# A one-core hybrid attention, pooling and expert layer: first norm by halves of tokens, activation table and token loads rearranged, five subtractions moved from VectorE to GpSimd

## The chip, the core and the metric

The kernel runs on one core of a Trainium2 chip. The metric is the device time of one execution in microseconds (us). An execution of the kernel before takes 1541.66 us (median of three). Five engines run side by side, each through its own queue in order: TensorE (PE in the profile, PEld its weight loads), VectorE (DVE), ScalarE (ACT), GpSimd (POOL) and SyncE (SP), which here issues nearly all transfers from memory.

## The reference

One layer for 512 tokens of 1024 channels. The opening of the kernel, where most of the change lies, computes the first norm, its modulation, and the first columns of one wide projection.

```python
def rms_norm(x, g):
    x32 = x.astype(jnp.float32)
    y = x32 * lax.rsqrt(jnp.mean(x32 * x32, axis=-1, keepdims=True) + EPS)
    return (y * g.astype(jnp.float32)).astype(x.dtype)
...
        ada = c @ w_ada[layer] + b_ada[layer]
        shift1, scale1, gate1, shift2, scale2, gate2 = [a[:, None, :] for a in jnp.split(ada, 6, axis=-1)]

        h = rms_norm(x, g_norm1[layer]) * (1.0 + scale1) + shift1
        z = h @ w_in[layer]
        zq, zk, zv, ziq, zik, ziw, zp, zg = jnp.split(z, cuts, axis=-1)
        q = rms_norm(zq.reshape(B, S, N_HEADS, HEAD_DIM), g_q[layer])
        k = rms_norm(zk, g_k[layer])
...
        mixed = (g_attn * y_attn + g_pool * y_pool) @ w_out[layer]
        x = x + gate1 * mixed

        h2 = rms_norm(x, g_norm2[layer]) * (1.0 + scale2) + shift2
        x = x + gate2 * peer_ffn(h2, w_peer_q[layer], peer_subkeys[layer], peer_u[layer], peer_v[layer])
```

In between stand sparse attention over 128 chosen keys, a pooling mixer with four windows, and, after the second norm, an expert lookup of 128 experts a token, which takes most of the time.

## The kernel before

Channels lie on the 128 partitions and tokens along the row: `x` is eight slices `xs[:, d, :]` of 128 channels by 512 tokens. A product in full precision is made of three passes of reduced-precision matmuls: each operand is split into a high part (ACT copies it into the shorter format, `split` L138, `modulate` L157) and a low part, which is the operand less its high part (DVE, L139, L158). `passes` (L171 to L173) multiplies high by high, high weights by low activations, and low weights by high activations.

The opening, with the names that the profile shows:

- SP loads `col`, `crow` and the eight slices of x (L249), then in turn two rows of `w_ada` (`wada`, L105) and one block of `w_in` (`ws`, L165), five times, then the remaining `wada`. Four buffers hold `wada`, three hold `ws`: the next transfer of a kind is issued when an earlier buffer has been used up.
- ACT squares each slice (`n1sq`, L144), DVE adds the squares up (`n1p`, L146), and PE sums over channels by a product with `ones` (`n1s`, L150 and L151; the eighth square goes to PE directly). A load of ACT's function table (L256) stands in ACT's queue ahead of the eighth square.
- `rsqrt` (L126) takes the root of the sum for all 512 tokens: three ACT functions (L129 to L131) and one refining step on DVE (L132 to L134) whose second instruction, L133, is a `tensor_scalar`.
- For each slice d DVE forms two columns of `ada` (L106, an instruction of 128x1024 that also sums, followed by a short read of its accumulator), adds the bias (L267), forms the gain `a1` (L268), the normed slice `n1f` (L156) and, after ACT has made the high part `hh` (L157), the low part `hl` (L158). While d is below five, DVE also forms the low part `wls` of the weight block that has come (L139).
- PE multiplies each finished slice with every block that has come: five blocks by eight slices by three passes, 120 matmuls of 128x512, in an order that a scheduler set when the kernel was built.

The scheduler places instructions on each engine by its own estimate of times, so the code does not tell the order; the rows of the next section but one do. Later parts call the same helpers: `rsqrt` for keys, queries and the second norm, `split` for all weight blocks, `square` and `modulate` for the second norm (L508 to L525).

## Time and profile before

| | |
|---|---|
| three executions | 1541.14, 1541.66, 1542.42 us |
| the profiled execution | 1543.48 us, of which the span from first to last instruction is 1541.7 us |
| mean granted clock of TensorE | 0.993 of full speed |
| busy | PE 97%, PEld 84%, DVE 84%, ACT 42%, POOL 21% of the span |

The page of a profile tells busy shares over the whole span. A stage is read with the table of busy time by stretches (a row has the stretch, its length, then PE, PEld, DVE, ACT and POOL), the timeline of one engine (start, duration, engine, line, operation, output and inputs, shapes, count, and in brackets how long the engine sat idle before and what ended that), and the chain of waits. On one engine the start of the next instruction less the start of this one is what an instruction costs; its duration is a little longer, since neighbours overlap at the ends.

### The profile page before, as it was taken

The page shows a single profiled execution, that of the slowest core. Times are in us where ns is not written, and L with a number is a line of the kernel's source. Part 1 is how long each engine was busy: PE and PEld are TensorE (multiplying, and loading weights), DVE is VectorE, ACT ScalarE, POOL GpSimd, SP SyncE. Part 2 cuts the span into 40 slices and gives each one's busy share as a digit, 9 for nine tenths or more (in the row PEclk, how much of TensorE's full clock was granted, in tenths as well). Part 3 has the DMA queues.
Part 4 walks back from the last instruction along what each step waited for, and adds up shares of the span by engine and source line. Part 5 has one row for each costly group of instructions (what it writes and reads, how often), then busy time and mean ns, then how long its engine had stood idle before and what let it go on. Part 6 is the DMA issues. An engine that isn't in the chain of part 4 may idle for free.

```text
span 1541.7 us, 22240 instructions
## 1 busy us (share of the span) xinstructions
PE 1497.2 (97%) x7889; PEld 1301.8 (84%) x7889; DVE 1294.3 (84%) x2672; ACT 647.2 (42%) x991; POOL 324.8 (21%) x318
## 2 busy tenths in 40 slices
PE   5999999999999999999999999999999999999998
PEld 3778787877789999899888999999999999998886
DVE  7799886767999999993778888888888888888887
ACT  4653555533444454453333333333333333333332
POOL 0000000000000000001123444444444444453320
PEclk8999999999999999999999999999999999999999
DMA  8412673523236666689889999999999999998884
GB/s 313 178 55 89 233 237 92 197 97 110 70 110 209 201 182 206 213 249 331 316 317 351 332 344 357 317 360 320 354 346 336 358 316 362 331 348 315 317 302 147
DMA packets 158545, 393.91 MB, mean 256 GB/s; under 512 B 13537, under 2 KB 68449, under 8 KB 158306
## 3 DMA queue, kind: packets, MB, share of 16 engines
q1 hardware_dynamic: 121570, 258.26, 48.1%
q0 software_dynamic: 36864, 134.23, 24.8%
q8 instruction: 62, 1.02, 0.3%
q14 instruction: 49, 0.40, 0.1%
HBM read 358.75 MB, written 33.69 MB: 255 GB/s over the span
## 4 chain that ended last, share of the span: by engine, by line
PE 79%; DVE 14%; DMA 3%; ACT 3%; issue 1%; SPq 0%; ACTq 0%; DVEq 0%
PE acc L807 31%; PE pse L556 6%; PE pse L555 6%; PE pse L554 6%; PE pse L570 4%; PE pse L572 4%; PE pse L571 3%; PE gm L667 3%; DMA v<-v 2%; DVE ule L534 2%; DVE bias L352 1%; PE po L471 1%; DVE m L351 1%; PE psga L173 1%; PE pso L171 1%
## 5 line engine op out<-in xcount | busy, mean ns | idle before, releaser
L732 POOL DMA_INDIRECT ur<-u,ei x128 | 156.6, 1224 | 605.5 <-DMA ad<-gelu 366.5
L807 PE MATMUL acc<-vl,Wh 128*128 128x512 f32 x768 | 237.1, 389 | 0.5 <-DVE vl L799 0.4
L807 PE MATMUL acc<-vh,Wl 128*128 128x512 f32 x768 | 237.3, 390 | 0.0
L807 PE MATMUL acc<-vh,Wh 128*128 128x512 f32 x768 | 236.6, 389 | 0.0
L740 POOL DMA_INDIRECT vr<-v,ei x128 | 165.2, 1290 | 213.7 <-DVE sacc L745 185.0
L799 DVE TENSOR_TENSOR vl<-v,vh 128x1024 fp32r<-128x1024 f32 x128 | 156.8, 1225 | 62.6 <-ACT vh L797 62.4
L556 PE MATMUL pse<-h2h,ule 128*128 128x384 f32 x552 | 185.2, 335 | 0.7 <-DVE ule L534 0.7
L554 PE MATMUL pse<-h2h,uhe 128*128 128x384 f32 x552 | 184.5, 334 | 1.2 <-ACT uhe L533 1.2
L555 PE MATMUL pse<-h2l,uhe 128*128 128x384 f32 x552 | 184.6, 334 | 0.0
L796 ACT ACTIVATE Wh<-gelu 128x384 fp32r<-128x384 f32 x106 | 55.6, 525 | 287.9 <-PE acc L807 170.2
L807 PEld LDWEIGHTS acc<-vl,Wh 128*128 128x128 f32 x768 | 143.9, 188 | 31.2 <-DVE vl L799 1.5
L807 PEld LDWEIGHTS acc<-vh,Wl 128*128 128x128 f32 x768 | 144.2, 188 | 30.0
L570 PE MATMUL pse<-h2h,uhe 128*128 128x384 f32 x472 | 168.2, 356 | 0.6 <-ACT gelu L579 0.6
L534 DVE TENSOR_TENSOR ule<-ue,uhe 128x1024 fp32r<-128x1024 f32 x128 | 156.0, 1218 | 15.2 <-ACT uhe L533 15.1
L572 PE MATMUL pse<-h2h,ule 128*128 128x384 f32 x472 | 161.6, 343 | 5.3 <-DVE ule L534 5.3
L745 DVE SCALAR_TENSOR_TENSOR sacc<-vr,wt,sacc 128x1024 f32<-128x1024 f32 x127 | 162.8, 1282 | 2.4
L807 PEld LDWEIGHTS acc<-vh,Wh 128*128 128x128 f32 x768 | 143.2, 188 | 24.5
L571 PE MATMUL pse<-h2l,uhe 128*128 128x384 f32 x472 | 159.2, 337 | 0.0
L533 ACT ACTIVATE uhe<-ue 128x1024 fp32r<-128x1024 f32 x128 | 134.5, 1051 | 58.4 <-PE pse L571 38.2
L734 DVE SCALAR_TENSOR_TENSOR ur<-ur,hx 128x1024 f32<-128x1024 f32 x128 | 150.8, 1220 | 0.9 <-DMA ur<-u,ei 0.9
L797 ACT ACTIVATE vh<-v 128x1024 fp32r<-128x1024 f32 x128 | 135.9, 1062 | 14.2 <-DMA v<-v 13.9
L554 PEld LDWEIGHTS pse<-h2h,uhe 128*128 128x128 f32 x552 | 103.6, 188 | 4.3 <-ACT uhe L533 1.7
(422 smaller groups left out, 2672.5 us busy)
## 6 DMA issues: line engine op xcount, KB each, us to landing
ue<-uT SPq DMA_DIRECT2D x128, 512.0 KB, 5.3
v<-v SPq DMA_DIRECT2D x128, 512.0 KB, 5.8
wada<-w_ada SPq DMA_DIRECT2D x48, 512.0 KB, 4.6
gd<-st SPq DMA_DIRECT2D x24, 1024.0 KB, 5.7
g<-gd SPq DMA_DIRECT2D x48, 512.0 KB, 8.0
ad<-gelu SPq DMA_DIRECT2D x22, 192.0 KB, 2.8
wgp<-w_in SPq DMA_DIRECT2D x8, 512.0 KB, 3.6
wga<-w_in SPq DMA_DIRECT2D x8, 512.0 KB, 4.4
```

The lines of the kernel that those rows point to most:

```text
L534: V.tensor_tensor(lo, src, hi.bitcast(F32), op=ALU.subtract)
L554: T.matmul(p, hi[:, k, :], h2h[:, k, :n], start=(k == 0), stop=False)
L555: T.matmul(p, hi[:, k, :], h2l[:, k, :n], start=False, stop=False)
L556: T.matmul(p, lo[:, k, :], h2h[:, k, :n], start=False, stop=(k == DT - 1))
L570: T.matmul(ps, hi[:, k, :], h2h[:, k, :ND], start=(k == 0), stop=False)
L571: T.matmul(ps, hi[:, k, :], h2l[:, k, :ND], start=False, stop=False)
L572: T.matmul(ps, lo[:, k, :], h2h[:, k, :ND], start=False, stop=(k == DT - 1))
L732: G.indirect_dma_start(out=ur, out_offset=None, in_=u, in_offset=bass.IndirectOffsetOnAxis(ap=ei3[:, k:k + 1], axis=0))
L740: G.indirect_dma_start(out=vr, out_offset=None, in_=v, in_offset=bass.IndirectOffsetOnAxis(ap=ei3[:, k:k + 1], axis=0))
L745: V.scalar_tensor_tensor(sacc, vr, wt[:, k:k + 1], sacc, op0=ALU.mult, op1=ALU.add)
L799: V.tensor_tensor(vl, vr, vh.bitcast(F32), op=ALU.subtract)
L807: T.matmul(acc[tb][i], x[:, t], y[:, i * 512:(i + 1) * 512], start=(c == 0 and n == 0), stop=(c == NEXP - 1 and n == 2))
```

## The change

Five things. The root of the first norm, its first modulated slice, and the last square are computed in two halves of 256 tokens (`CUT1 = 2`; `CUT2 = 1` leaves the second norm whole). The function table of the first norm is asked for at the start of ACT's queue instead of ahead of the eighth square, so that one load stands where two stood. x comes in four transfers of two slices each, from an array that the host lays out for it, in the opening and again ahead of the second norm. `rsqrt` loses its `tensor_scalar`: the factor it applied is multiplied into the gains in `col` once, at the start, by two small instructions (and into the factor that scales the queries' roots). And `load` takes an engine for the low part: for the first five blocks of `w_in` it is GpSimd.

```diff
--- before.py
+++ after.py
 SCALED = 14
+CUT1 = 2
+CUT2 = 1
...
+        V.tensor_scalar(col[:, C_G1:C_GQ], col[:, C_G1:C_GQ], -0.5 / D, None, op0=ALU.mult)
+        V.tensor_scalar(col[:, C_GK:C_GIK + 1], col[:, C_GK:C_GIK + 1], -0.5 / 64, None, op0=ALU.mult)
...
+        def pieces(n, cut):
+            return [slice(i * n // cut, (i + 1) * n // cut) for i in range(cut)]
+
+        def rsqrt(ps, scale, name, tag="rs", n=S, cut=1):
 
             r = tmp.tile([P, n], F32, tag=f"{tag}_r", name=f"{name}r", bufs=1)
             t = tmp.tile([P, n], F32, tag=f"{tag}_t", name=f"{name}t", bufs=1)
-            A.activation(t, ps, AF.Ln, bias=eps, scale=scale)
-            A.activation(r, t, AF.Exp, scale=-0.5)
-            A.activation(t, r, AF.Square)
-            V.scalar_tensor_tensor(t, ps, EPS / scale, t, op0=ALU.add, op1=ALU.mult)
-            V.tensor_scalar(t, t, -0.5 * scale, 1.5, op0=ALU.mult, op1=ALU.add)
-            V.tensor_tensor(r, r, t, op=ALU.mult)
+            for c in pieces(n, cut):
+                A.activation(t[:, c], ps[:, c], AF.Ln, bias=eps, scale=scale)
+                A.activation(r[:, c], t[:, c], AF.Exp, scale=-0.5)
+                A.activation(t[:, c], r[:, c], AF.Square)
+                V.scalar_tensor_tensor(t[:, c], ps[:, c], EPS / scale, t[:, c], op0=ALU.add, op1=ALU.mult)
+                V.scalar_tensor_tensor(r[:, c], t[:, c], -3.0 / scale, r[:, c], op0=ALU.add, op1=ALU.mult)
             return r
 
-        def split(hi, lo, src):
+        def split(hi, lo, src, engine=V):
             A.activation(hi, src, AF.Copy)
-            V.tensor_tensor(lo, src, hi.bitcast(F32), op=ALU.subtract)
+            engine.tensor_tensor(lo, src, hi.bitcast(F32), op=ALU.subtract)
 
         def square(part, src, d, name):
 
             sq = tmp.tile([P, S], F32, tag="sq", name=f"{name}{d}") if d else part
             A.activation(sq, src, AF.Square)
-            if 0 < d < DT - 1:
+            if d:
                 V.tensor_tensor(part, part, sq, op=ALU.add)
-            return sq
-
-        def square_sum(ps, part, last):
-            T.matmul(ps, ones, part, start=True, stop=False)
-            T.matmul(ps, ones, last, start=False, stop=True)
-
-        def modulate(src, rs, ga, shift, hi, lo, name):
+
+        def square_sum(ps, part, src, name, cut=1):
+
+            sq = tmp.tile([P, S], F32, tag="sq", name=name)
+            for c in pieces(S, cut):
+                A.activation(sq[:, c], src[:, c], AF.Square)
+                T.matmul(ps[:, c], ones, part[:, c], start=True, stop=False)
+                T.matmul(ps[:, c], ones, sq[:, c], start=False, stop=True)
+
+        def modulate(src, rs, ga, shift, hi, lo, name, cut=1):
 
             f = tmp.tile([P, S], F32, tag="nf", name=name)
-            V.scalar_tensor_tensor(f, src, ga, rs, op0=ALU.mult, op1=ALU.mult)
-            A.activation(hi, f, AF.Identity, bias=shift)
-            V.scalar_tensor_tensor(lo, f, shift, hi.bitcast(F32), op0=ALU.add, op1=ALU.subtract)
-
-        def load(src, kt, name, pool=wp):
+            for c in pieces(S, cut):
+                V.scalar_tensor_tensor(f[:, c], src[:, c], ga, rs[:, c], op0=ALU.mult, op1=ALU.mult)
+                A.activation(hi[:, c], f[:, c], AF.Identity, bias=shift)
+                V.scalar_tensor_tensor(lo[:, c], f[:, c], shift, hi[:, c].bitcast(F32), op0=ALU.add, op1=ALU.subtract)
+
+        def load(src, kt, name, pool=wp, engine=V):
 
             w = wp.tile([P, DT, P], F32, tag="w", name=f"w{name}")[:, :kt, :]
             hi = pool.tile([P, DT, P], F32R, tag="wh", name=f"wh{name}", bufs=2)[:, :kt, :]
             lo = pool.tile([P, DT, P], F32R, tag="wl", name=f"wl{name}", bufs=2)[:, :kt, :]
             nc.sync.dma_start(out=w, in_=src)
-            split(hi, lo, w)
+            split(hi, lo, w, engine)
             return hi, lo
...
                 xs = xp.tile([P, DT, S], F32, name="xs")
+                tc.keep_in_program_order(A.preload_act_table_set("natural_log_exp_and_others"))
                 crow = wp.tile([P, D], F32, tag="wa", name="crow", bufs=3)[0:1, :]
                 nc.sync.dma_start(out=crow, in_=cvec)
                 ps = pst.tile([P, S], F32, name="n1s")
                 part = tmp.tile([P, S], F32, tag="nf", name="n1p")
                 for d in range(DT):
-                    nc.sync.dma_start(out=xs[:, d, :], in_=xT[d])
-                    sq = square(part, xs[:, d, :], d, "n1sq")
-                square_sum(ps, part, sq)
+                    if d % 2 == 0:
+                        nc.sync.dma_start(out=xs[:, d:d + 2, :], in_=xT[d // 2])
+                    if d < DT - 1:
+                        square(part, xs[:, d, :], d, "n1sq")
+                square_sum(ps, part, xs[:, DT - 1, :], "n1sq7", CUT1)
                 for i in range(2):
                     cp = pst.tile([P, S], F32, name=f"cp{i}")
                     T.matmul(cp, ones[0:1, :], crow[:, i * S:(i + 1) * S], start=True, stop=True)
                     A.copy(cb[:, i * S:(i + 1) * S], cp)
-                tc.keep_in_program_order(A.preload_act_table_set("natural_log_exp_and_others"))
                 both = lambda t, d: t.rearrange("p (i d) -> p i d", d=DT)[:, :, d]
                 rs, ws, accs = None, [], []
                 for d in range(DT):
                     for j in (DT + d, d):
                         ada_col(j, xp, 4)
                     if d < len(begin):
-                        ws.append(load(w_in[begin[d][0]], DT, f"s{d}", (wp, xp, xp, xq, xq)[d]))
+                        ws.append(load(w_in[begin[d][0]], DT, f"s{d}", (wp, xp, xp, xq, xq)[d], G))
                         accs.append(pst.tile([P, S], F32, name=f"ps{d}"))
                     if rs is None:
-                        rs = rsqrt(ps, 1.0 / D, "n1")
+                        rs = rsqrt(ps, 1.0 / D, "n1", cut=CUT1)
                     V.tensor_tensor(both(ada[:, 0:16], d), both(ada[:, 0:16], d), both(col[:, C_BADA:C_BADA + 16], d), op=ALU.add)
                     V.scalar_tensor_tensor(a1[:, d:d + 1], ada[:, DT + d:DT + d + 1], 1.0, col[:, C_G1 + d:C_G1 + d + 1],
                                            op0=ALU.add, op1=ALU.mult)
-                    modulate(xs[:, d, :], rs, a1[:, d:d + 1], ada[:, d:d + 1], hh[:, d, :], hl[:, d, :], f"n1f{d}")
+                    modulate(xs[:, d, :], rs, a1[:, d:d + 1], ada[:, d:d + 1], hh[:, d, :], hl[:, d, :], f"n1f{d}", 1 if d else CUT1)
                     for b in range(len(accs)):
                         for k in range(d + 1) if b == d else (d,):
...
             rq = rsqrt(qn, 1.0 / 64, "nq", "rq", TB * NH)
-            V.tensor_scalar(rq, rq, 0.125, None, op0=ALU.mult)
+            V.tensor_scalar(rq, rq, -0.5 / 64 * 0.125, None, op0=ALU.mult)
...
-        for d in range(DT):
-            nc.sync.dma_start(out=xs[:, d, :], in_=xT[d])
+        for d in range(0, DT, 2):
+            nc.sync.dma_start(out=xs[:, d:d + 2, :], in_=xT[d // 2])
...
             ps = linear(f"o{j}", yh, yl)
-            V.scalar_tensor_tensor(xs[:, j, :], ps, ada[:, 16 + j:17 + j], xs[:, j, :], op0=ALU.mult, op1=ALU.add)
-            sq = square(part, xs[:, j, :], j, "n2sq")
-        square_sum(sums, part, sq)
-        rs = rsqrt(sums, 1.0 / D, "n2")
+            for c in pieces(S, CUT2 if j == DT - 1 else 1):
+                V.scalar_tensor_tensor(xs[:, j, c], ps[:, c], ada[:, 16 + j:17 + j], xs[:, j, c], op0=ALU.mult, op1=ALU.add)
+            if j < DT - 1:
+                square(part, xs[:, j, :], j, "n2sq")
+        square_sum(sums, part, xs[:, DT - 1, :], "n2sq7", CUT2)
+        rs = rsqrt(sums, 1.0 / D, "n2", cut=CUT2)
+
+        def second(d, cut=1):
+            modulate(xs[:, d, :], rs, a2[:, d:d + 1], ada[:, 24 + d:25 + d], h2h[:, d, :], h2l[:, d, :], f"n2f{d}", cut)
+
+        second(0, CUT2)
...
-        "xT": np.ascontiguousarray(x[0].T).reshape(DT, P, S),
+        "xT": np.ascontiguousarray(x[0].T.reshape(DT // 2, 2, P, S).transpose(0, 2, 1, 3)),
```

VectorE, first norm. Before, the rows behind the first two `wada` (`n1t` and `n1r` are the root, `wls` low parts of weights):

```order
L267 TENSOR_TENSOR ada<-ada,col 128x2
L268 SCALAR_TENSOR_TENSOR a_61<-ada,col 128x1
L139 TENSOR_TENSOR wls_180<-ws_178,whs_179 128x1024
L106 SCALAR_TENSOR_TENSOR wada_202,ada<-wada_202,cb 128x1024
L132 SCALAR_TENSOR_TENSOR n1t<-n1s,n1t 128x512
L106 SCALAR_TENSOR_TENSOR wada_205,ada<-wada_205,cb 128x1024
L133 TENSOR_SCALAR n1t<-n1t 128x512
L267 TENSOR_TENSOR ada<-ada,col 128x2
L134 TENSOR_TENSOR n1r<-n1r,n1t 128x512
L139 TENSOR_TENSOR wls_210<-ws_208,whs_209 128x1024
L156 SCALAR_TENSOR_TENSOR n1f_195<-xs,a_61,n1r 128x512
L268 SCALAR_TENSOR_TENSOR a_61<-ada,col 128x1
```

After, from the same place:

```order
L281 TENSOR_TENSOR ada<-ada,col 128x2
L141 SCALAR_TENSOR_TENSOR n1t<-n1s,n1t 128x256
L282 SCALAR_TENSOR_TENSOR a_61<-ada,col 128x1
L142 SCALAR_TENSOR_TENSOR n1r<-n1t,n1r 128x256
L168 SCALAR_TENSOR_TENSOR n1f_200<-xs,a_61,n1r 128x256
L111 SCALAR_TENSOR_TENSOR wada_210,ada<-wada_210,cb 128x1024
L141 SCALAR_TENSOR_TENSOR n1t<-n1s,n1t 128x256
L170 SCALAR_TENSOR_TENSOR hl<-n1f_200,ada,hh 128x256
L142 SCALAR_TENSOR_TENSOR n1r<-n1t,n1r 128x256
L111 SCALAR_TENSOR_TENSOR wada_213,ada<-wada_213,cb 128x1024
L168 SCALAR_TENSOR_TENSOR n1f_200<-xs,a_61,n1r 128x256
L281 TENSOR_TENSOR ada<-ada,col 128x2
```

The root, the normed slice and its low part now stand there twice at half width, the two `wls` and the `tensor_scalar` are gone, and the first half of the normed slice stands ahead of the second half of the root.

VectorE, end of the opening, before (`wlq` is the low part of the sixth weight block; the two `n1f` are slices six and seven of zero to seven):

```order
L158 SCALAR_TENSOR_TENSOR hl<-n1f_358,ada,hh 128x512
L268 SCALAR_TENSOR_TENSOR a_61<-ada,col 128x1
L106 SCALAR_TENSOR_TENSOR wada_407,ada<-wada_407,cb 128x1024
L156 SCALAR_TENSOR_TENSOR n1f_385<-xs,a_61,n1r 128x512
L267 TENSOR_TENSOR ada<-ada,col 128x2
L139 TENSOR_TENSOR wlq_433<-wq_431,whq_432 128x1024
L158 SCALAR_TENSOR_TENSOR hl<-n1f_385,ada,hh 128x512
L268 SCALAR_TENSOR_TENSOR a_61<-ada,col 128x1
L156 SCALAR_TENSOR_TENSOR n1f_412<-xs,a_61,n1r 128x512
```

After:

```order
L111 SCALAR_TENSOR_TENSOR wada_412,ada<-wada_412,cb 128x1024
L282 SCALAR_TENSOR_TENSOR a_61<-ada,col 128x1
L111 SCALAR_TENSOR_TENSOR wada_415,ada<-wada_415,cb 128x1024
L168 SCALAR_TENSOR_TENSOR n1f_393<-xs,a_61,n1r 128x512
L281 TENSOR_TENSOR ada<-ada,col 128x2
L282 SCALAR_TENSOR_TENSOR a_61<-ada,col 128x1
L168 SCALAR_TENSOR_TENSOR n1f_420<-xs,a_61,n1r 128x512
L147 TENSOR_TENSOR wlq_441<-wq_439,whq_440 128x1024
L170 SCALAR_TENSOR_TENSOR hl<-n1f_393,ada,hh 128x512
L170 SCALAR_TENSOR_TENSOR hl<-n1f_420,ada,hh 128x512
```

The normed slice seven, its `ada` and its gain `a` now stand ahead of the low part `hl` of slice six, one right behind the other, and `wlq` stands behind them.

GpSimd, opening, before (`ends` and `pz` are constants and a margin of zeros, the rest serves the expert lookup):

```order
L222 MEMSET ends 128x32
L224 MEMSET ends 64x1 x8
L326 MEMSET pz 128x4x16
L877 MEMSET pk_begin 128x8
L878 MEMSET pk_step 128x8
```

After:

```order
L234 MEMSET ends 128x32
L236 MEMSET ends 64x1 x8
L147 ISA
L147 TENSOR_TENSOR wls_181<-ws_179,whs_180 128x1024
L147 TENSOR_TENSOR wls_218<-ws_216,whs_217 128x1024
L147 TENSOR_TENSOR wls_246<-ws_244,whs_245 128x1024
L147 TENSOR_TENSOR wls_280<-ws_278,whs_279 128x1024
L147 TENSOR_TENSOR wls_320<-ws_318,whs_319 128x1024
L340 MEMSET pz 128x4x16
```

Five subtractions of 128x1024 stand in a queue that was empty there, with one set-up instruction ahead of them.

## Rows read from the trace of the kernel before

**Rows 1.** The page's first part: busy us, share of the span, instructions.

```profile
PE 1497.2 (97%) x7889; PEld 1301.8 (84%) x7889; DVE 1294.3 (84%) x2672; ACT 647.2 (42%) x991; POOL 324.8 (21%) x318
```

**Rows 2.** Stretches: busy us (instructions) by engine, granted clock, DMA share, GB/s.

```profile
25.00:30.00 5.00, 5.00 (x13) 3.55 (x13) 5.00 (x10) 1.78 (x2) 0.00 (x0) 0.55 0.83 292
30.00:35.00 5.00, 4.33 (x19) 3.19 (x18) 5.00 (x10) 1.67 (x2) 0.00 (x0) 1.00 0.66 233
45.00:50.00 5.00, 5.00 (x22) 3.61 (x21) 5.00 (x10) 1.24 (x2) 0.00 (x0) 1.00 0.97 382
```

**Rows 3.** Timeline of DVE, opening: start, duration, line, operation, output<-inputs, shapes, idle before.

```profile
8.94 3.08 DVE L146 TENSOR_TENSOR n1p<-n1p,n1sq 128x512 f32<-128x512 f32 x4 [0.31 <-ACT n1sq L144]
...
14.45 0.16 DVE L267 TENSOR_TENSOR ada<-ada,col 128x2 f32<-128x2 f32 x1
14.64 0.16 DVE L268 SCALAR_TENSOR_TENSOR a<-ada,col 128x1 f32<-128x1 f32 x1
15.55 1.23 DVE L139 TENSOR_TENSOR wls<-ws,whs 128x1024 fp32r<-128x1024 f32 x1 [0.74 <-ACT whs L138]
...
17.94 0.69 DVE L132 SCALAR_TENSOR_TENSOR n1t<-n1s,n1t 128x512 f32<-128x512 f32 x1
18.55 1.22 DVE L106 SCALAR_TENSOR_TENSOR wada<-wada,cb 128x1024 f32<-128x1024 f32 x1
...
19.69 0.42 DVE L133 TENSOR_SCALAR n1t<-n1t 128x512 f32<-128x512 f32 x1
...
20.14 0.69 DVE L134 TENSOR_TENSOR n1r<-n1r,n1t 128x512 f32<-128x512 f32 x1
20.75 1.22 DVE L139 TENSOR_TENSOR wls<-ws,whs 128x1024 fp32r<-128x1024 f32 x1
21.89 0.74 DVE L156 SCALAR_TENSOR_TENSOR n1f<-xs,a,n1r 128x512 f32<-128x512 f32 x1
22.55 0.15 DVE L268 SCALAR_TENSOR_TENSOR a<-ada,col 128x1 f32<-128x1 f32 x1
22.62 1.22 DVE L106 SCALAR_TENSOR_TENSOR wada<-wada,cb 128x1024 f32<-128x1024 f32 x1
...
49.64 0.74 DVE L158 SCALAR_TENSOR_TENSOR hl<-n1f,ada,hh 128x512 fp32r<-128x512 f32 x1
```

**Rows 4.** Timeline of ACT, opening: squares, table load, first step of the root.

```profile
7.28 0.63 ACT L144 ACTIVATE n1sq<-xs 128x512 f32<-128x512 f32 x1 [1.32 <-DMA xs<-xT]
...
11.11 1.28 ACT L256 ACT_TABLE_LOAD   x1
...
15.89 0.69 ACT L129 ACTIVATE n1t<-n1s,eps 128x512 f32<-128x512 f32 x1 [0.38 <-PE n1s L151]
```

**Rows 5.** Timeline of PE, opening: first product of the blocks, last two.

```profile
23.44 1.22 PE L171 MATMUL ps<-hh,whs 128*128 128x512 f32 x2 [7.58 <-ACT hh L157]
...
55.97 0.39 PE L172 MATMUL ps<-hl,whs 128*128 128x512 f32 x1
56.20 0.40 PE L173 MATMUL ps<-hh,wls 128*128 128x512 f32 x1
```

**Rows 6.** Chain of waits at the second norm: start, us, what.

```profile
338.41 0.44 DVE n2t L133
```

**Rows 7.** Timeline of POOL, one round of the expert stage.

```profile
1002.04 1.68 POOL L732 DMA_INDIRECT ur<-u,ei  x1 [3.87 <-DVE ur L734]
1004.02 0.94 POOL L732 DMA_INDIRECT ur<-u,ei  x1 [0.30 <-issue]
```

**Rows 8.** Timeline of DVE in the same round.

```profile
1001.69 1.22 DVE L734 SCALAR_TENSOR_TENSOR ur<-ur,hx 128x1024 f32<-128x1024 f32 x1
...
1002.83 1.22 DVE L734 SCALAR_TENSOR_TENSOR ur<-ur,hx 128x1024 f32<-128x1024 f32 x1
```

**Rows 9.** POOL by line: shapes, count, busy us, mean ns of one, idle before.

```profile
L326 POOL MEMSET pz<- 128x64 f32 x1 | 0.2, 158 | 54.5 <-PE ps L172 54.5
L222 POOL MEMSET ends<- 128x32 f32 x1 | 0.1, 125 | 0.3 <-POOLq L1032 0.3
```

More of the change, by code (lines that the diff above doesn't have):

```diff
@@ L523, in layer @@
             nc.sync.dma_start(out=x2d[tb], in_=xo)
-        for d in range(DT):
-            modulate(xs[:, d, :], rs, a2[:, d:d + 1], ada[:, 24 + d:25 + d], h2h[:, d, :], h2l[:, d, :], f"n2f{d}")
+        for d in range(1, DT):
+            second(d)
     up = ctx.enter_context(tc.tile_pool(name="up", bufs=2, side="right", reuse_waits="tile"))
```

1 line of the change is left out of this document (removed).

## The prediction

> **What bounds the kernel now.** I read the page's busy shares first, then the table of stretches for the opening, then the engines' timelines there, and last the expert stage for what POOL and DVE do to each other. Over the span PE is busy 97% [rows 1], so the kernel ends earlier only where PE stands still or runs slowly, and the opening is one such place. PE's first product of the weight blocks starts at 23.44 us after 7.58 us of idling, and the last ends a step after 56.20 [rows 5]. In the stretches from 25 us on DVE is busy 5.00 of 5.00 us, while DMA has a share to spare in two of the three [rows 2]. So DVE sets the pace of the opening: it forms the normed slices, and PE takes them as they come. At the end of the opening this is exact. The low part of slice six starts at 49.64 and lasts 0.74, to 50.4 [rows 3]. From its first product on PE's order holds 25 matmuls to the end of the blocks; at 0.23 each (55.97 to 56.20 [rows 5]) that is 5.8, and 50.4 + 5.8 = 56.2 is where the blocks end. In the changed order 25 matmuls stand behind that low part too. So I follow DVE from the end of the squares' sum (8.94 + 3.08 = 12.0) to this low part, 37.6 us, and let the rest of the kernel move with it: behind the opening I found no work that starts at a fixed time, each transfer waiting for a buffer.
>
> **What leaves DVE.** Five `wls` subtractions: one occupies DVE from 20.75 to 21.89, 1.14, so 5.7. The wait of 0.74 ahead of the first of them. The `tensor_scalar`, 0.4. The full-width steps of the root, 17.94 to 18.55 = 0.61 each for two, and of the first slice, 21.89 to 22.55 = 0.66 each for two: 2.5 [rows 3]. Together 9.3.
>
> **What comes to DVE.** Eight instructions of half width. From 512 to 1024 elements the cost grows from 0.61 to 1.14, so 256 elements save about half of 0.53: 0.35 for a step of the root, 0.40 for one of the slice, 4 x 0.35 + 4 x 0.40 = 3.0. The first of them must wait for ACT. At full width the sum over channels reaches ACT at 15.89 [rows 4], 3.9 after DVE's last add; half of it is ready after half the time, near 14.0, three ACT steps of some 0.4 (the full step is 0.69) end near 15.2, and DVE, done with two `wada` and one small instruction, would come to it at 14.6: some 0.7 of waiting, and 0.3 more where a half waits for the step just before it. Then the small instructions. In the new order the bias, the gain `a` and the normed slice stand directly behind one another, each needing the one before. A dependent step takes 0.19 (14.45 to 14.64), a free one 0.07 (22.55 to 22.62) [rows 3], so 0.12 is lost each time; counting the rows for slices one to seven I find 15 such places, 1.8. Last, slice seven and its gain now stand ahead of the low part of slice six: 0.66 + 0.07 = 0.7. Together 3.0 + 1.0 + 1.8 + 0.7 = 6.5. DVE by itself gains 9.3 - 6.5 = 2.8.
>
> **x, and the table.** The table load, 1.28 on ACT ahead of the last square [rows 4], goes. It stood behind the seventh square, so it held the eighth alone; the root then waited for PE, which multiplied the other part first (2 us from 12.0). Hence no second gain for the load, it is in the halves. Four transfers of two slices: slice two comes with slice three. ACT already sits idle 1.32 for slice two, to 7.28 [rows 4], and five adds of 3.08/4 = 0.77 [rows 3] follow at best back to back, so waiting for the pair delays the sum if the larger transfers move no faster. I put 0.5 of loss, from 1.0 of gain to 1.0 of loss. The same exchange ahead of the second norm is covered by the output projection: nothing.
>
> **Elsewhere.** The second norm's chain runs through the `tensor_scalar` at 338.41, 0.44 [rows 6]: 0.4 gained. In the norms of keys and queries it stands beside PE's work: nothing, at most 0.8 for two. The two factors multiplied into `col` run while DVE waits for the first square. PE's clock averages 0.55 of full from 25 to 30 us and 1.00 from 30 on [rows 2], after the 7.58 of idling; PE will idle there again (an estimate: 2 less, as its first slice comes in halves), and start at the lower level (1.2 GHz, not 2.4). Since DVE sets the end, this costs nothing unless it lasts some microseconds longer. So without GpSimd's share the sum is -2.8 + 0.5 - 0.4 = -2.7.
>
> **What GpSimd makes of it.** The trace has no POOL subtraction. Below, its price is DVE's own, 1.14. For more, the two zero fills: 64 elements take 158 ns, 32 take 125 [rows 9], so 1.03 ns an element for one stream and 0.09 fixed. Two streams read one after the other make 0.09 + 2 x 1.06 = 2.2 for 1024 elements; three, with the write, 3.3. I take 2.2, since the fill shows a stream's pace and this operation reads two. By itself that is hidden: POOL stands empty, and five blocks in the 40 us of the opening leave each more than that. But it may not run beside DVE. In the expert stage the POOL instruction at 1002.04 takes 1.68, the next one, at 1004.02, 0.94 [rows 7]. The difference is 0.74, and 1002.04 + 0.74 = 1002.78: just where DVE's instruction from 1001.69 ends and the next, from 1002.83, begins [rows 8]. Both DVE instructions read two tensors from SBUF. So a POOL instruction was kept out until DVE's was over, and got in between two. That one reads a column of numbers and let DVE go on at once; a subtraction reads for 2 us. If the exclusion holds both ways, DVE stands still for each: every large instruction of DVE here reads two tensors. Lower bound nothing, upper bound the whole POOL time. I take the whole, since the row shows exclusion for a whole instruction and not a sharing of pace, less 0.2 each for what falls into DVE's own small waits: 5 x 2.0 = 10.0.
>
> The Trainium skill's page "SBUF — State Buffer", section "Who interferes with whom", says that a VectorE instruction with two SBUF inputs and a GpSimd instruction that reads SBUF exclude each other, the one that comes second being blocked until the first is over; rows 7 and 8 agree for one direction (0.74 us of waiting), and no row here shows the other. By it the result is this forecast, and without it the first rival. "GPSIMD Engine Reference", section "3.1 Elementwise — side-by-side cycle accounting", gives 4497 ns for 2048 elements; an estimate from it is 2.25 for 1024, and the sum would be 0.25 longer.
>
> **The forecast.** The profiled execution takes 1543.48, its span 1541.7, 1.8 around it; the median of 1541.66 is 1.8 below it. The change acts inside the span, so I put it on the median. -2.7 + 10.0 = +7.3: **1549.0**. With 1.14 for a subtraction it is 5 x 0.94 - 2.7 = +2.0, 1543.7; with 3.3, +12.8, 1554.5. Its own range is 1544 to 1552.
>
> **Rivals.** *GpSimd runs beside DVE.* The five subtractions are off DVE and nothing stands still: 1538.96, say 1539.0, between 1537.7 (x earlier by 1.0) and 1540.5. For it: DVE's two instructions in rows 8 keep their 1.22 while POOL works. Against it: the 0.74. It turns the sign: below 0.5 of standstill per subtraction the change is a gain. *POOL waits and DVE does not.* DVE goes on, and POOL gets only the gaps; a subtraction then takes as long as a gap takes to come, 4 to 5.5. PE's order has 66 matmuls behind the first low part of the fifth block; 66 x 0.23 = 15.2. With 5.5 each from 16.3 (an estimate: the first `wls` starts at 15.55 once its high part is ready, and a set-up instruction precedes it) the fifth is ready at 43.8 and the blocks end at 59.0, 2.8 later than now; with 4 they end by DVE, 2.7 earlier. So 1539 to 1544.5, middle 1541.7. PE would then wait for POOL in the third pass. *The low clock lasts.* Each further us at 1.2 GHz costs PE half of one; as DVE sets the end, part of that is hidden; I allow up to 1.5 more in either case. It widens the ranges.
>
> **How the numbers follow.** Forecast 0.56, first rival 0.30, second 0.14. About 0.2%, 3.1 us, is what a measurement can tell here from no change, so the bounds are 1538.6 and 1544.7. The forecast lies above 1544.7 with 0.51 of its 0.56. The first rival lies around its lower bound: 0.14 faster, 0.16 same. The second: 0.01 faster, 0.10 same, 0.03 slower. Fast tails that I can't place, an order that falls out better at 70 to 160 us, give the first rival's side 0.03. Faster 0.18, same 0.28, slower 0.54. Both signs hold much, so the range spans both: 1538.0 to 1552.0, which leaves out about 0.08 on each side.
>
> **What would show it.** Forecast: the five POOL rows last 1.2 to 3.3, DVE's `wada`, `n1f` or `hl` beside them start late or last 2 to 3.5 instead of 1.22 and 0.74, slice six's low part starts near 57 (49.64 - 2.8 + 0.5 + 10.0), and the blocks end near 64. First rival: all DVE rows keep their length, and that low part starts near 47.3. Second: DVE keeps its lengths, POOL's rows last 4 or more, and PE's third pass waits for POOL. The second norm's chain without `tensor_scalar`, 0.4 shorter, shows that term. It is wrong if the end of the opening moves and the end of the kernel does not.

## The result, and the profile after

| | before | after |
|---|---|---|
| executions | 1541.14 to 1542.45 us (four) | 1549.82, 1552.02, 1553.95, 1554.08 us |
| median | 1542.04 us | 1552.99 us |
| span of the profiled execution | 1541.7 us | 1552.3 us |
| mean granted clock | 0.993 | 0.992 |

The ratio is 1.0069, 95% interval 1.0055 to 1.0083: 10.95 us slower by the medians, 10.6 by the two spans. The forecast was 1549.0, 7.3 slower, and its range ended at 1552.0. The mechanism that it put first is in the trace; the size was not.

The page's first part of the changed kernel, to be read beside [rows 1], and three stretches beside [rows 2]:

```profile
PE 1501.3 (97%) x7893; PEld 1307.4 (84%) x7893; DVE 1299.1 (84%) x2668; ACT 645.5 (42%) x995; POOL 340.0 (22%) x323
```

```profile
25.00:30.00 5.00, 3.39 (x7) 2.14 (x8) 4.93 (x11) 2.18 (x3) 1.26 (x1) 1.00 0.64 239
30.00:35.00 5.00, 2.72 (x12) 1.93 (x11) 4.90 (x8) 1.29 (x2) 1.41 (x1) 1.00 0.49 183
45.00:50.00 5.00, 5.00 (x23) 4.04 (x22) 4.90 (x10) 0.72 (x1) 0.03 (x1) 1.00 0.45 166
```

The shares of the span hardly move, and DVE still looks full in the opening. What it is full of is seen one row at a time. The timeline of DVE (start, duration, line, operation, output and inputs):

```profile
16.85 0.42 DVE L141 SCALAR_TENSOR_TENSOR n1t<-n1s,n1t 128x256 f32<-128x256 f32 x1 [2.79 <-ACT n1t L140]
...
18.17 3.37 DVE L111 SCALAR_TENSOR_TENSOR wada<-wada,cb 128x1024 f32<-128x1024 f32 x1
...
21.48 0.41 DVE L141 SCALAR_TENSOR_TENSOR n1t<-n1s,n1t 128x256 f32<-128x256 f32 x1
21.81 2.22 DVE L170 SCALAR_TENSOR_TENSOR hl<-n1f,ada,hh 128x256 fp32r<-128x256 f32 x1
...
29.08 3.41 DVE L111 SCALAR_TENSOR_TENSOR wada<-wada,cb 128x1024 f32<-128x1024 f32 x1
...
35.40 1.22 DVE L111 SCALAR_TENSOR_TENSOR wada<-wada,cb 128x1024 f32<-128x1024 f32 x1
...
36.66 2.21 DVE L281 TENSOR_TENSOR ada<-ada,col 128x2 f32<-128x2 f32 x1
...
42.84 2.22 DVE L281 TENSOR_TENSOR ada<-ada,col 128x2 f32<-128x2 f32 x1
...
54.90 1.23 DVE L111 SCALAR_TENSOR_TENSOR wada<-wada,cb 128x1024 f32<-128x1024 f32 x1 [0.62 <-DMA wada<-w_ada]
...
58.90 1.41 DVE L170 SCALAR_TENSOR_TENSOR hl<-n1f,ada,hh 128x512 fp32r<-128x512 f32 x2
```

And the timeline of POOL over the same time:

```profile
17.91 5.83 POOL L147 TENSOR_TENSOR wls<-ws,whs 128x1024 fp32r<-128x1024 f32 x2 [15.99 <-ACT whs L146]
28.74 2.67 POOL L147 TENSOR_TENSOR wls<-ws,whs 128x1024 fp32r<-128x1024 f32 x1 [4.99 <-ACT whs L146]
35.46 3.39 POOL L147 TENSOR_TENSOR wls<-ws,whs 128x1024 fp32r<-128x1024 f32 x1 [4.05 <-ACT whs L146]
41.63 3.40 POOL L147 TENSOR_TENSOR wls<-ws,whs 128x1024 fp32r<-128x1024 f32 x1 [2.78 <-ACT whs L146]
```

Five POOL subtractions, and five DVE rows that are too long: a `wada` of 3.37 and one of 3.41, where others of its kind take 1.22; a half `hl` of 2.22, where the other half takes 0.48; two additions of two columns of 2.21 and 2.22, which take 0.16 elsewhere. The excess, in the order of the starts, is 2.15 + 1.74 + 2.19 + 2.05 + 2.06 = 10.2 us. The rows also show who waits for whom. The POOL row of 35.46 ends at 38.85, and so does DVE's addition (36.66 + 2.21 = 38.87). The `wada` of 35.40, ahead of that addition, ends at 36.6: POOL, issued at 35.46, sat out that `wada` for 1.15 and then worked for 2.24, and DVE sat out the 2.24. So a POOL row's duration holds its waiting, and the 2.2 to 2.25 behind it is the work.

At the end of the opening, PE's last product of the five blocks and the first of the next one (`psq`):

```profile
65.41 0.39 PE L185 MATMUL ps<-hh,wls 128*128 128x512 f32 x1
65.64 0.40 PE L183 MATMUL psq<-hh,whq 128*128 128x512 f32 x1
```

Before, the last stood at 56.20 [rows 5], and `psq` began at 56.44:

```profile
56.44 0.39 PE L171 MATMUL psq<-hh,whq 128*128 128x512 f32 x1
```

The opening ends 9.2 later. Below, "the blocks' end" is always the start of that first `psq` product.

At the second norm the chain of waits goes from `n2t` straight to `n2r`; the `tensor_scalar` of [rows 6] is gone, and the shift against the kernel before (how much later a row starts than the same row there) shrinks there by 0.5:

```profile
347.92 0.64 DVE n2t L141
348.56 0.02 issue
348.59 0.70 DVE n2r L142
```

### The profile page after: what moved, and what is told of

Read it like the earlier page. It is cut to its first block, busy times and chain, and to the rows that moved or that the text cites. A ratio compares the mean times of both kernels' runs of the same rounds, so it can differ in the third digit from the quotient of the medians.

```text
span 1552.3 us, 22243 instructions
## 1 busy us (share of the span) xinstructions
PE 1501.3 (97%) x7893; PEld 1307.4 (84%) x7893; DVE 1299.1 (84%) x2668; ACT 645.5 (42%) x995; POOL 340.0 (22%) x323
## 4 chain that ended last, share of the span: by engine, by line
PE 84%; DVE 7%; DMA 3%; ACT 2%; issue 0%; SPq 0%; ACTq 0%; DVEq 0%
PE acc L828 30%; PE pse L577 6%; PE pse L576 6%; PE pse L575 6%; PE pse L591 4%; PE pse L593 4%; PE pse L592 4%; PE gm L688 3%; DMA v<-v 1%; DVE ule L555 1%; PE po L485 1%; PE pso L183 1%; PE pso L184 1%; PE psgp L185 1%; PE psgp L184 1%; PE psga L185 1%
## 5 line engine op out<-in xcount | busy, mean ns | idle before, releaser
L554 ACT ACTIVATE uhe<-ue 128x1024 fp32r<-128x1024 f32 x128 | 134.5, 1051 | 58.1 <-PE pse L592 39.8
L819 DVE TENSOR_TENSOR Wl<-gelu,Wh 128x384 fp32r<-128x384 f32 x106 | 59.3, 559 | 57.2 <-ACT Wh L817 51.4
```

## The experiments

I held three theories. PORT: a POOL subtraction keeps DVE out for its whole work, and this is the loss. REST: GpSimd is about neutral, and the halves, the smaller pieces and their order are the loss. ALL: everything else in the change is the gain that it was meant to be. The ratio is always to the kernel before on the same chip.

| run | what it is | median, us | ratio (95%) | blocks' end, us |
|---|---|---|---|---|
| | the kernel before | 1541.4 to 1542.9 | 1 | 56.4 |
| | the changed kernel | 1553.0 | 1.0069 (1.0055 to 1.0083) | 65.6 |
| all_but_pool | change, low parts on DVE | 1543.6 | 1.0010 (1.0001 to 1.0020) | 57.9 |
| pool_alone | before, low parts on GpSimd | 1548.7 | 1.0049 (1.0036 to 1.0062) | 63.8 |
| no_halves | change, norm at full width | 1551.4 | 1.0060 (1.0043 to 1.0077) | 67.6 |
| no_halves_no_pool | change with neither | 1543.3 | 1.0011 (1.0003 to 1.0020) | 58.1 |
| subtractions_twice | before, five POOL subtractions added | 1551.6 | 1.0071 (1.0057 to 1.0086) | 68.9 |
| zero_fills | before, 30 POOL fills added | 1541.6 | 1.0004 (0.9994 to 1.0014) | 56.5 |
| two_banks | all_but_pool, sum's halves in two banks | 1541.1 | 0.9996 (0.9985 to 1.0008) | 57.6 |
| two_banks_with_pool | change, sum's halves in two banks | 1549.8 | 1.0048 (1.0029 to 1.0066) | 66.0 |
| block_ahead_of_root | no_halves_no_pool, first low part ahead of the root | 1540.1 | 0.9992 (0.9983 to 1.0002) | 55.5 |
| block_ahead_again | the same | 1542.0 | 0.9994 (0.9982 to 1.0006) | 56.3 |
| first_block_ahead | no_halves_no_pool, the same program | 1541.4 (one) | none | 58.0 |
| fold_alone | before, without the `tensor_scalar` | 1541.3 | 1.0001 (0.9990 to 1.0011) | 56.7 |

The blocks' end is read from one execution of each. For the one kernel of block_ahead_of_root and block_ahead_again it is 55.5 and 56.3, so differences under 0.8 in that column show nothing by themselves.

### GpSimd taken out, and GpSimd alone

The first edit undoes one word of the change:

```diff
-                        ws.append(load(w_in[begin[d][0]], DT, f"s{d}", (wp, xp, xp, xq, xq)[d], G))
+                        ws.append(load(w_in[begin[d][0]], DT, f"s{d}", (wp, xp, xp, xq, xq)[d]))
```

> The changed kernel with the five low parts back on DVE; halves, table, x and the fold stay. In the trace of the changed kernel five DVE rows beside a POOL subtraction are 10.2 us longer in sum than their like (3.37 for 1.22, 2.22 for 0.48, 3.41 for 1.22, 2.21 and 2.22 for 0.16). Theory PORT (these 10.2 us are the loss, the rest costs a little): the standstill goes (-10.2), five subtractions of 1.14 come back (+5.7), the wait of 0.62 for a late wada goes: the end of the blocks moves from 65.6 to about 60, the time from 1553 to 1543 to 1548. Which end depends on whether the 2.79 us that DVE waits for the first half of the root stay (order: they stay, the first subtraction stands behind them). Rival REST (POOL is about neutral; the halves, the smaller pieces and their order are the loss): 1550 to 1553, blocks end near 65. Rival ALL (everything else in the change is a gain as it was meant): 1539 or below.

Measured: 1543.6, ratio 1.0010, blocks' end 57.9. Every long DVE row is gone. Of the 9.2 of the opening 1.5 is left. It is PORT, at the low end of what was expected: the excess and the late `wada` go, and the blocks end 2.1 earlier still than the 60 I had written. Order can account for that (an estimate, not tested by itself): with the low parts back in DVE's queue other work stands between the small dependent steps again, and for that order the prediction has 1.8 + 0.7. ALL is out with this run and with no_halves_no_pool below, since both medians lie above the kernel before and not below it.

The second edit makes that one change alone in the kernel before (the helper `split` takes an engine, and `load` hands it on):

```diff
-                        ws.append(load(w_in[begin[d][0]], DT, f"s{d}", (wp, xp, xp, xq, xq)[d]))
+                        ws.append(load(w_in[begin[d][0]], DT, f"s{d}", (wp, xp, xp, xq, xq)[d], nc.gpsimd))
```

> The kernel before with the engine of the five low parts alone changed to GpSimd. PORT: DVE loses 5 x 1.14 and the wait of 0.74 ahead of the first, and gains five standstills of about 2.05: -6.4 + 10.2 = +3.8, near 1546 (1544 to 1548), with five DVE rows about 2 us longer than their like. REST: no change or a gain, 1538 to 1542. ALL: as PORT, or more: the whole +11, 1550 to 1553.

Measured: 1548.7, ratio 1.0049. Its timeline of DVE, three of the five long rows:

```profile
15.74 3.35 DVE L106 SCALAR_TENSOR_TENSOR wada<-wada,cb 128x1024 f32<-128x1024 f32 x1 [0.94 <-DMA wada<-w_ada]
...
35.30 2.27 DVE L268 SCALAR_TENSOR_TENSOR a<-ada,col 128x1 f32<-128x1 f32 x1
...
41.34 2.22 DVE L267 TENSOR_TENSOR ada<-ada,col 128x2 f32<-128x2 f32 x1
```

The sign and the mechanism are PORT's; the size is 7.4 at the blocks' end where I had written 3.8. The five excesses are 2.0 to 2.2 each, as expected. What I had left out is the order (read from the trace and priced, not tested by itself): with the low parts gone from DVE's queue the scheduler set bias, gain and slice directly behind one another and the gain of slice seven ahead of slice six's low part, as it does in the changed kernel, where I had priced this at 1.8 + 0.7, and there is a new wait of 0.94 for a transfer. 3.8 + 2.5 + 0.9 = 7.2. Taken together the two runs bracket it: adding GpSimd to the kernel before costs 7.4 in the opening, taking it from the changed kernel gives back 7.7.

### The price of one subtraction by itself

In `subtractions_twice` DVE keeps its five low parts and its order, and POOL computes the same five into a tile that nobody reads (`raw` holds the blocks as they came):

```diff
+                idle = xq.tile([P, DT, P], F32, name="idle")
...
+                        nc.gpsimd.tensor_tensor(idle, raw[-1], ws[-1][0].bitcast(F32), op=ALU.subtract)
                         accs.append(pst.tile([P, S], F32, name=f"ps{d}"))
```

> The kernel before, whose DVE still takes the five low parts, with five POOL subtractions of the same operands added whose result nobody uses. DVE's order is that of the kernel before. PORT: the pure price of a subtraction: each holds one DVE instruction for 2.0 to 2.3, five times, +10 to +11.5, of which the wait of 0.74 and PE's reserve hide up to 1.5: 1550 to 1553.5. Rival RELIEF (DVE stands still only where what it does next needs the very data that POOL reads, or is free of it): 1542 to 1545.

Measured: 1551.6, ratio 1.0071. Its timeline of DVE, three of the five long rows:

```profile
17.85 3.37 DVE L106 SCALAR_TENSOR_TENSOR wada<-wada,cb 128x1024 f32<-128x1024 f32 x1
...
33.18 2.81 DVE L158 SCALAR_TENSOR_TENSOR hl<-n1f,ada,hh 128x512 fp32r<-128x512 f32 x1
...
43.16 2.34 DVE L273 SCALAR_TENSOR_TENSOR a<-ada,col 128x1 f32<-128x1 f32 x1
```

The five excesses are 1.5 to 2.2 each and sum to 10.1. DVE's low part of slice six starts 11.2 later than in [rows 3], of which 1.0 is a squares' sum that ended 1.0 later in this execution. (The blocks end 12.4 later: here PE is busy without a gap from 55 us on, and no longer waits for that low part.) Nothing was relieved, DVE's instructions and their order are those of the kernel before, and the subtractions cost 2.0 us of DVE each on average. This is the plainest reading of the price: 2 us of DVE to save 1.14 of DVE.

`zero_fills` asks what it is in a POOL instruction that keeps DVE out. It adds 30 fills, which write 128x1024 and read nothing:

```diff
+                idle = xq.tile([P, DT, P], F32, name="idle")
...
+                        for i in range(6):
+                            nc.gpsimd.memset(idle, 0.0)
                         accs.append(pst.tile([P, S], F32, name=f"ps{d}"))
```

> The kernel before with 30 POOL zero fills of 128x1024 in the opening, from 2 to about 35 us, which write and read nothing; at 1.03 ns an element 1.1 us each. Theory READS (only a POOL instruction that reads SBUF keeps DVE out): no DVE row longer than its like (wada 1.22), 1541 to 1543. Rival ANY (every POOL instruction that touches SBUF keeps DVE out): DVE gets in only between fills, its rows of 8 to 35 us grow by about 1 each, 1555 or more.

Measured: 1541.6, ratio 1.0004, blocks' end 56.5. The timelines of POOL and of DVE in this run:

```profile
2.83 29.39 POOL L266 MEMSET idle<- 128x1024 f32 x29
```

```profile
16.57 1.22 DVE L106 SCALAR_TENSOR_TENSOR wada<-wada,cb 128x1024 f32<-128x1024 f32 x1
...
19.46 0.75 DVE L133 TENSOR_SCALAR n1t<-n1t 128x512 f32<-128x512 f32 x1
...
20.85 1.22 DVE L139 TENSOR_TENSOR wls<-ws,whs 128x1024 fp32r<-128x1024 f32 x1
```

For 29.4 us POOL writes without a gap, 1.01 us a fill, and DVE's rows that read two tensors keep their length, the large ones their 1.22. So POOL's writing costs those rows nothing; the subtraction also reads, and by this difference it is the reading that keeps them out (a POOL instruction that reads one tensor was not run). One row did grow: the `tensor_scalar`, which reads a single tensor, takes 0.75 for the 0.42 of [rows 3]. Writing alone is thus not free for every DVE instruction. This is one row, and no run asks why. The DVE side of the rule is in the changed kernel: at 21.48 `n1t<-n1s,n1t` takes its 0.41, undelayed. It reads one tensor from PSUM and one from SBUF, and POOL is then at work on the second of the two subtractions listed from 17.91 (that pair ends at 23.74, and the work takes 2.2). The `hl` behind it reads two tensors from SBUF and stands until 23.5. That POOL was already at work at 21.48 is worked out from its end, since one row holds the pair.

The Trainium skill, "SBUF — State Buffer", section "Who interferes with whom", states it in this form: DVE with two SBUF inputs contends with a GpSimd instruction that reads SBUF, and not with one that only writes. Five long rows in each kernel with the subtractions, and none that reads two tensors beside 29.4 us of fills, agree with it.

### The halves

```diff
-CUT1 = 2
+CUT1 = 1
```

> The changed kernel with CUT1 = 1: the first norm at full width, the low parts still on GpSimd. PORT: the five standstills stay; eight half instructions (3.0) become four whole ones (2.5), the root comes when the whole sum has come, as it does now too, since ACT began the first half at 15.45, only when PE had finished both halves: -1 to +0.5, so 1552 to 1553.5. REST: the halves are the loss, 1543 to 1546.

> The changed kernel with neither halves nor GpSimd: table, x in four transfers, the fold and the order that the scheduler makes of them are left. PORT: the squares' sum ends 0.44 earlier (11.58 for 12.02), the fold saves 0.4 at the first and 0.4 at the second norm, but in this order the root stands ahead of the first subtraction and of the third wada, so DVE waits about 3.4 us for ACT where before it worked: about +1, 1541 to 1543.5. ALL: a gain of 1 to 2, 1540 to 1541. REST: 1545 or more.

Measured: 1551.4 and 1543.3, ratios 1.0060 and 1.0011. With GpSimd the halves move slice six's low part from 59.45 to 58.90, and the blocks' end from 67.6 to 65.6, of which about 1.4 is PE's clock: no_halves has a granted clock of 0.67 from 60 to 65 us, the changed kernel 1.00. Without GpSimd they move the blocks' end from 58.1 to 57.9. The medians of the two pairs differ by 1.6 and 0.2, the halves on the slower side, with intervals that overlap. REST is out: the halves are not the loss. They are hardly a gain either, and the traces of ACT and PE in the changed kernel tell why:

```profile
10.82 0.72 ACT L160 ACTIVATE n1sq<-xs 128x256 f32<-128x256 f32 x2 [0.17 <-DVE n1p L154]
15.45 0.47 ACT L138 ACTIVATE n1t<-n1s,eps 128x256 f32<-128x256 f32 x1 [3.91 <-PE n1s L162]
```

```profile
12.65 1.06 PE L162 MATMUL n1s<-n1sq,ones 128*128 128x256 f32 x2
13.50 1.06 PE L161 MATMUL n1s<-n1p,ones 128*128 128x256 f32 x2
14.36 1.06 PE L162 MATMUL n1s<-n1sq,ones 128*128 128x256 f32 x2
```

PE multiplies the first half from 11.63 to about 13.7 and the second until 15.4. ACT takes the first half at 15.45, when both are done, so the first half of the root comes as late as the whole did. The halves lie in one PSUM tile of 512 columns, one bank, and I took it that the program makes a reader wait until PE has finished with the bank. The Trainium skill, "PSUM — Partial Sum Buffer", section "PSUM bank collisions raise a hardware error", has the rule that such guards are set by bank and not by address; the start at 15.45 agrees with it.

Two PSUM tiles test that (`half` picks the tile of a half, in the products, in ACT's first step and in DVE's first):

```diff
-                ps = pst.tile([P, S], F32, name="n1s")
+                ps = [pst.tile([P, S], F32, tag=t, name=n) for t, n in (("n1s", "n1s"), ("ps4", "n1u"))]
...
-                T.matmul(ps[:, c], ones, part[:, c], start=True, stop=False)
-                T.matmul(ps[:, c], ones, sq[:, c], start=False, stop=True)
+                T.matmul(half(ps, c), ones, part[:, c], start=True, stop=False)
+                T.matmul(half(ps, c), ones, sq[:, c], start=False, stop=True)
```

> The changed kernel with the low parts on DVE, and the two halves of the squares' sum in two PSUM tiles (two banks) in place of one. Theory BANK (ACT reads the first half late because PE still writes the other half into the same bank, and the program makes it wait): ACT's first step of the root starts near 13.7, when the first half's products end, where it started at 15.4 with one bank; the order then runs both halves through ACT back to back; DVE's wait of 2.79 falls to about 1 and a second one of about 1 comes; 0.5 to 1.5 less than with one bank, 1542 to 1543, blocks end near 57 instead of 57.9. Rival PE (the half products themselves end late, since a product of 256 columns costs nearly what one of 512 does): ACT still starts at 15 or later, 1543.5.

Measured: 1541.1, ratio 0.9996, blocks' end 57.6. The timelines of ACT and DVE:

```profile
13.82 0.47 ACT L141 ACTIVATE n1t<-n1s,eps 128x256 f32<-128x256 f32 x1 [2.21 <-PE n1s L165]
...
15.53 0.47 ACT L141 ACTIVATE n1t<-n1u,eps 128x256 f32<-128x256 f32 x1 [0.34 <-PE n1u L165]
```

```profile
15.22 0.42 DVE L144 SCALAR_TENSOR_TENSOR n1t<-n1s,n1t 128x256 f32<-128x256 f32 x1 [1.28 <-ACT n1t L143]
...
16.93 0.42 DVE L144 SCALAR_TENSOR_TENSOR n1t<-n1u,n1t 128x256 f32<-128x256 f32 x1 [1.21 <-ACT n1t L143]
```

That the shared tile held ACT back is shown: ACT starts 1.5 earlier, at 13.82, near the 14.0 of the forecast. Two tiles are also two banks, so this run does not tell which of the two the guard goes by. But the wait of 2.79 only splits into 1.28 and 1.21, and the blocks' end moves by 0.3, less than two executions of one kernel can differ. The median is 2.5 below that of all_but_pool, far more than the opening moved; the section on the prediction says where else the total moves. With GpSimd:

> The changed kernel whole, the low parts on GpSimd, with the two halves of the squares' sum in two PSUM tiles. ACT starts the first half near 13.8 and the second near 15.5 (as in two_banks). In the trace of two_banks the end of the blocks came only 0.33 earlier by it, since DVE then waited 1.28 and 1.21 in place of 2.79. PORT: the five standstills stay, blocks end 0.3 to 2.5 earlier than the changed kernel's 65.64, 63 to 65.3; the time stays 7 to 11 above the kernel before. Rival (the shared bank, not GpSimd, makes most of the loss): 1545 or less.

Measured: 1549.8, ratio 1.0048, blocks' end 66.0. The blocks' end did not come earlier, as I had expected, but 0.3 later. The rival, that the bank makes most of the loss, is out.

### What is left without GpSimd

In all_but_pool and no_halves_no_pool DVE waits about 3 us for the root (2.79 and 3.24). The scheduler set the root ahead of the first block's low part and of the third `wada`, which the kernel before does in that time. The fold does not do that (fold_alone keeps the old order); I put it down to the early table, but the table and the four transfers of x were not tested apart. Here the low part is held ahead of it, in ACT's queue and in DVE's:

```diff
-            split(hi, lo, w, engine)
+            for i in split(hi, lo, w, engine):
+                if name == "s0":
+                    tc.keep_in_program_order(i)
...
-                A.activation(t[:, c], ps[:, c], AF.Ln, bias=eps, scale=scale)
+                i = A.activation(t[:, c], ps[:, c], AF.Ln, bias=eps, scale=scale)
+                if name == "n1":
+                    tc.keep_in_program_order(i)
```

> The changed kernel with the low parts on DVE and the norm at full width (as no_halves_no_pool), and with the first block's low part held ahead of the root in ACT's and DVE's queues, where the kernel before has it. Theory ORDER (what is left of the loss is DVE's wait of 3.24 for ACT, since the early table made the scheduler put the root first): the wait falls under 1, the blocks end near 56.4 - 0.4 - 0.4 = 55.6 (before 56.44; sum 0.44 earlier, fold 0.4), the second norm is 0.4 shorter, time 1 to 1.5 below the kernel before: 1540 to 1541. Rival SPELLS (the rest is PE's low clock after waits, not the order): no lower than no_halves_no_pool, 1543.

> block_ahead_of_root once more, to narrow its interval: the opening ends 1.0 earlier than in the kernel before and the second norm is 0.5 shorter in its trace, so 1.5 below the kernel before, a ratio near 0.999.

Measured: 1540.1 and 1542.0, ratios 0.9992 and 0.9994. The wait for the root in no_halves_no_pool and in this kernel, from their timelines of DVE:

```profile
17.52 0.69 DVE L141 SCALAR_TENSOR_TENSOR n1t<-n1s,n1t 128x512 f32<-128x512 f32 x1 [3.24 <-ACT n1t L140]
```

```profile
14.27 1.23 DVE L150 TENSOR_TENSOR wls<-ws,whs 128x1024 fp32r<-128x1024 f32 x1 [0.20 <-ACT whs L150]
...
17.30 0.69 DVE L143 SCALAR_TENSOR_TENSOR n1t<-n1s,n1t 128x512 f32<-128x512 f32 x1 [0.66 <-ACT n1t L142]
```

ORDER holds in the trace: the wait falls to 0.66, and the blocks' end comes 2.6 and 1.8 earlier than in no_halves_no_pool, 1.0 and 0.2 earlier than in the kernel before. Both ratios lie below one, and both intervals reach over it: this is the best version I have, and it is not shown to beat the kernel before. The fold alone,

> The kernel before with the fold alone (no tensor_scalar in the root, the factor in the gains): DVE's order at the root is the same as before but for that row. 0.4 in the opening and 0.4 at the second norm: 0.8 below the kernel before, 1540.5 to 1542. Rival: nothing, since what stands behind on DVE waits for ACT or a transfer there.

gave 1541.3, ratio 1.0001: the 0.5 at the second norm is in its trace (the shift goes from 0.0 to -0.5 there), the 0.4 of the opening does not show at the blocks' end (56.7), and the total can't be told from nothing. The 0.8 that I had expected is not in the time.

## Why the prediction was right in its mechanism and short in its size

Each term of its sum for DVE's path to slice six's low part, against the trace of the changed kernel:

| term | forecast | trace |
|---|---|---|
| standstills | +10.0 | +10.2 (the five long rows) |
| what leaves and comes, without waits | -3.8 | -3.9 (the remainder) |
| waiting for the first half of the root | +1.0 | +2.8 (the 2.79 at 16.85) |
| squares' sum, by x and the table | +0.5 | -0.4 (ends at 11.58, not 12.02) |
| a `wada` that arrives late | 0 | +0.6 (the 0.62 at 54.90) |
| start of that low part | 57.3 | 58.9 |

**Right.** The choice between the rivals, which rested on 0.74 us of waiting in one POOL row [rows 7, 8], its extension to the other direction, the price of 2.2 for a subtraction from the fill's pace of one stream (fills of 1024 elements now take 1.01 us, 0.99 ns an element), and the count of DVE's rows, whose -3.9 is what is left when the rest is taken off and was not measured by itself. What is behind the opening did move with it: the shift is about 8.2 to 9.2 from 60 to 270 us. The choice stood on one row of POOL, thin ground that held. The price is borne out as a number (2.2 to 2.25); that two tensors are read one after the other, each at the fill's pace, no run shows.

**Wrong, the halves.** The step that failed is "half of it is ready after half the time, near 14.0, three ACT steps of some 0.4 (the full step is 0.69) end near 15.2", with "some 0.7 of waiting" behind it. PE's half is ready in time. I had not asked who else uses the tile that ACT reads: ACT waits for both halves, and DVE for 2.79. With two tiles `two_banks` has ACT at 13.82 and its three steps done at 15.2, as forecast, and DVE still waits 1.28 + 1.21, since it came at 13.9 and not at 14.6 and had nothing placed between the halves. So the term was put at 1.0, with two tiles it would be 2.5, and it was 2.8.

**Wrong, smaller.** For x I reckoned with a loss, and the squares' sum ended 0.4 earlier; without these 0.9 the opening would have been 2.4 longer than forecast, not 1.5. How much of it is x is open: the sum ends at 11.4 to 12.0 in the kernels with four transfers and at 11.7 to 13.0 in those with eight. I had no term for transfers that come late behind the moved order, 0.6. PE's start at the lower level does not show in the granted clock, which is 1.00 from 25 to 30 us; its price was put at nothing.

**Wrong, the rest of the kernel.** Between the blocks' end and the last instruction I had -0.4. The fold gave its 0.5, and yet the span grew from 9.2 to 10.6. In the table of stretches the granted clock falls at 270 to 280, 345 to 355 and 425 to 437 us of the changed kernel, where the kernel before shows 1.00. The changed kernel, then two of the same stretches before:

```profile
270.00:280.00 10.00, 8.81 (x35) 6.33 (x34) 2.72 (x5) 3.02 (x6) 0.00 (x0) 0.83 0.19 52
345.00:355.00 10.00, 7.76 (x39) 6.04 (x38) 8.75 (x14) 6.66 (x11) 0.00 (x0) 0.83 0.54 212
425.00:437.00 12.00, 9.30 (x36) 8.58 (x36) 12.00 (x73) 4.38 (x6) 0.00 (x0) 0.72 0.26 89
```

```profile
270.00:280.00 10.00, 10.00 (x45) 8.08 (x44) 8.35 (x14) 5.29 (x10) 0.00 (x0) 1.00 0.27 79
345.00:355.00 10.00, 9.23 (x38) 6.59 (x39) 7.61 (x12) 5.52 (x8) 1.72 (x48) 1.00 0.24 92
```

In a spell at the lower level (1.2 GHz) one product of the changed kernel follows another after 0.43 instead of 0.23 us:

```profile
276.56 0.63 PE L183 MATMUL psua<-aTh,whua 128*128 128x512 f32 x1
276.99 0.63 PE L184 MATMUL psua<-aTl,whua 128*128 128x512 f32 x1
```

A spell adds up to 1.5: the shift goes from 8.7 to 10.2 across 275. In each place PE had just stood still for some tenths to two microseconds (waits of 0.5 to 2.2). The kernel before has such spells at 455 and 630 (granted clock 0.66 from 455 to 460 and 0.76 from 630 to 637), where the changed one has 1.00 or a later one. So the change is not needed for them. first_block_ahead is one more execution of the program of no_halves_no_pool, and the same places read so, first and second execution:

```profile
270.00:280.00 10.00, 10.00 (x40) 8.00 (x39) 5.78 (x10) 3.98 (x7) 0.00 (x0) 0.90 0.19 52
...
630.00:637.00 7.00, 5.28 (x35) 4.03 (x34) 7.00 (x15) 2.63 (x4) 0.00 (x0) 0.77 0.51 185
```

```profile
270.00:280.00 10.00, 10.00 (x45) 8.10 (x44) 6.98 (x11) 4.55 (x9) 0.00 (x0) 1.00 0.28 74
...
630.00:637.00 7.00, 5.81 (x64) 5.08 (x64) 7.00 (x13) 3.32 (x7) 0.00 (x0) 1.00 0.57 181
```

One program, blocks' end 58.1 and 58.0, spans of 1543.2 and 1539.6. So which of PE's waits are followed by a slow spell differs from execution to execution, and this moves the total by several microseconds.

The spells are not all of it. From 700 to 830 us, with a granted clock of 1.00, PE is busy 129.19 and 127.70 us and gets through 611 and 595 products in two executions of one program (block_ahead_of_root and block_ahead_again), and the first goes from 0.2 us behind the second to 2.7 ahead of it:

```profile
700.00:830.00 130.00, 129.19 (x611) 111.49 (x610) 89.91 (x128) 50.72 (x68) 27.63 (x26) 1.00 0.94 338
```

```profile
700.00:830.00 130.00, 127.70 (x595) 108.27 (x593) 88.49 (x126) 47.92 (x64) 26.58 (x25) 1.00 0.92 328
```

two_banks_with_pool, whose opening ends as late as the changed kernel's (66.0 and 65.6), has a span of 1547.2, 5.1 shorter. It is 2.1 ahead at 690 us, having a granted clock of 1.00 in the three stretches above, and 5.1 ahead at 850, with no spell of either kernel in between. What PE waits for there was not followed up. Whether the changed kernel meets more of either on average, as its median suggests, or met more in four executions, stays open.

**The steps that failed, in sum.** The forecast lies 4.0 below the median. One part is the 1.0 of waiting for the first half of the root, which measured 2.8; with the smaller terms the opening came out 1.5 longer than forecast. The other is the -0.4 behind the opening, where the spans show +1.4; its causes are those of the two paragraphs above, and their shares are open. The range had no term for the second part: I built it from the terms of the opening, beside three executions of the kernel before that lay 1.3 us apart; the many since lie between 1538.9 and 1548.1, 4.6 either way.

## What to carry to other kernels

Before work is moved from VectorE to GpSimd, look at what VectorE does meanwhile: where its instructions read two tensors from SBUF, GpSimd's reading time is VectorE's standing time, and here the trade was about 2 us lost for 1.14 saved, however empty GpSimd's queue was. Work cut in halves flowed here only when each half had a PSUM tile of its own, and gained only what the engines behind could do between them; in one tile the wait that ended the whole showed up again, unchanged, ahead of the first half. And where a scheduler orders the queues, the effect of an edit is read in the order that comes out: here the root came to stand ahead of 2.3 us of work that used to fill the wait.
